# Pairing the value products of two branches, and laying the compression inputs out by a token's place in its stretch of 16

## The chip, the cores and the metric

The kernel runs on one core of a Trainium2 chip. The metric is the device time of one execution in microseconds (us). Three runs of the kernel before gave 1453.22, 1454.13 and 1451.1 us, a median of 1453.22.

## The reference, cut to what matters

The program is a decoder trunk of two layers over 512 tokens of width 1024, in float32. Layer 0 mixes tokens with sparse attention in three branches, layer 1 with a recurrence (RWKV-7). Each layer also attends to 256 memory tokens and ends with a SwiGLU feed-forward block. The change touches three places of it:

```python
def _compress(kv, pos, w1, w2):            # keys (kvi 0) and values (kvi 1)
    S = kv.shape[1]
    n_cmp = (S - CMP_BLOCK) // CMP_STRIDE + 1          # 31 blocks of 32 tokens, a step of 16
    idx = jnp.arange(n_cmp)[:, None] * CMP_STRIDE + jnp.arange(CMP_BLOCK)[None, :]
    blocks = kv[:, idx] + pos[None, None, :, None, :]
    hid = jax.nn.gelu(jnp.einsum('bnlgd,lde->bnge', blocks, w1))
    return jnp.einsum('bnge,ed->bngd', hid, w2)
...
        o_s = jnp.einsum('bgrqk,bgqkd->bqgrd', p_s.astype(vg.dtype), vg)   # selected branch
...
        o_w = jnp.einsum('bgrqk,bkgd->bqgrd', p_w.astype(vwc.dtype), vwc)  # window branch
...
    return jnp.einsum('bhsm,bmhd->bshd', p, v).reshape(B, S, MEM_WIDTH)    # memory attention
```

## The kernel before, in words

All large matrix products have a weight tile of 128x128 on the array and 512 token columns streaming through; each is done three times with operands split into a high and a low part (`pm` tiles; `nxh`, `wsp` and the like are those parts). Products that are not split are plain float32 and appear in the trace as two rows per product.

The program is first recorded as a list of operations with their dependences; `schedule` then simulates the engines with fixed costs (the function `cost`) and picks, engine by engine, the ready operation with the lowest number that fits in the buffers. What comes out is a fixed order for each engine: on the chip an engine executes its list strictly in that order. All operations carry line 517, where the list is emitted, so rows are told apart by tile names. `flex` operations may go to ScalarE (ACT) or VectorE (DVE), whichever the scheduler finds free first. The field `after` of an operation adds dependences that the data doesn't ask for. For TensorE (PE) the scheduler also knows how much of the array an operation uses (`colmode`: 128 or 64 columns) and prefers to stay in a mode within the bounds of `TILED`.

Layer 0 (`nsa`) works in four groups of three heads. For each group and each query tile `qt` of 128 tokens, the two branches `br` (selected, window) get their scores (`pa<-kh,qs` and `pa<-kl,qs`), bias and minimum on DVE, the exponential on ACT, the normalization on GpSimd (POOL, tile `p`); then PE transposes `p` (`ptr<-cf,p`), an eviction copies the transposes from PSUM to `ap` in SBUF (`copied`), and the value products follow (`po<-ap,vst`): 64 output rows, 384 columns, with `tile_position=(0, 64*br)`, so branch 0 uses columns 0 to 63 of the array and branch 1 columns 64 to 127. There are qt+1 key tiles, so 2, 4, 6 or 8 value products, 80 in all four groups (160 rows). In the recorded program the two branches of a key tile stand beside each other, but each of them waits only for its own eviction. `mem_attn` has the same shape with 512 columns: per head pair m, two key tiles with two heads each, products `pa<-mpt,mvs` (64 output rows, heads on the two halves of the array); it runs four times, twice in each layer, 16 products.

The compression (`compress`) runs twice, for keys (kvi 0) and values (kvi 1). For each of two weight tiles m, a large product `pm` is evicted to `kcf` on DVE (two head groups of 64 rows, 512 tokens), and DMAs issued by SyncE's queue (SP) copy it into `kc2`: rows 0 to 63 hold a group's tokens, rows 64 to 127 the same shifted by one token, 8 DMAs per compression. Sixteen products `pa<-kc,wraw` (128x128 weights from `cw1`) read every 16th column: 128 columns for the 4 groups of 32 stretches and one column of positions, 129 in all, written by POOL from `cpos`. The `cost` function doubles the price of float32 products with 129 columns. Then follow the GELU (`cgt`), the second product (`cw`), and the block-diagonal copies (`cdi`).

Of the kernel before, what the change touches and what calls it, by code (L numbers as in the profile page):

```python
# [11 lines left out]
F32 = mybir.dt.float32  # L12
# [3 lines left out]
ALU = mybir.AluOpType  # L16
# [545 lines left out]
def cost(eng, meth, args, kw, outs, ins):  # L562
# [8 lines left out]
    if eng == "tensor":  # L571
# [5 lines left out]
        if x.dt == F32:  # L577
            t = n * 4 / 2.4 + 5
            if n == 129:
                t *= 2  # L580
            if m <= 64 and w.shape[0] <= 64:
                t = 58.0 if n <= 64 else 55.0
            elif n <= 64 and m <= 64:
                t = 54.0 if m > 32 else 27.0
            elif n >= 256 and m == 64:
                t = n * 2 / 2.4 + 5
            elif n < 128:
                t = max(t, 215.0 if m > 64 else 112.0 if m > 32 else 60.0)
        elif x.dt == F32R:
            t = n / 2.4 + 13  # L590
        else:
            t = n / 2.4 + 2 if m > 64 else 16
# [27 lines left out]
class B:  # L620
# [205 lines left out]
    def copied(self, out, ps):  # L826
        self.nc.flex(("scalar", "copy", (out, ps), {}), ("vector", "tensor_copy", (out, ps), {}))
# [21 lines left out]
    def mem_attn(self, m, qm, kv, ot):  # L849
# [31 lines left out]
        for mt in range(2):  # L881
            pts = []
            for i in range(2):
# [6 lines left out]
                self.copied(pts[i], pt)  # L890

            for i in range(2):
                nc.tensor.matmul(po[64 * i:64 * i + 64], vs[mt][:, 2 * m + i], pts[i],
                                 start=mt == 0, stop=mt == 1, tile_position=(0, 64 * i))
# [67 lines left out]
    def nsa(self, xt):  # L962
# [37 lines left out]
        def compress(kvis):  # L1000

            for kvi in kvis:


                flat = nc.tile([128, 2080], F32, "kc2", "kc2", 1)
                kc2 = flat[:, 0:2048].rearrange("p (g n) -> p g n", g=4)
                cpos = self.sm("cpos", [128, 16])
                nc.sync.dma_start(cpos, self.a["cpos"][kvi])
                nc.gpsimd.tensor_scalar(out=flat[:, 2048:2080:2], in0=cpos, scalar1=1.0,
                                        scalar2=1.0, op0=ALU.mult, op1=ALU.mult)  # L1010
                for m in range(2):
# [3 lines left out]
                    nc.vector.tensor_tensor(out=kcf, in0=ps, in1=R, op=ALU.mult)  # L1015
                    for half in range(2):
                        hs = slice(64 * half, 64 * half + 64)
                        g = 2 * m + half
                        nc.sync.dma_start(kc2[0:64, g, :], kcf[hs])
                        nc.sync.dma_start(kc2[64:128, g, 0:511], kcf[hs, 1:512])  # L1020
                ps = self.ax_ps()
                for c in range(2):
                    cw = self.wraw(self.a["cw1"][kvi][:, c * 1024:c * 1024 + 1024])
                    for l in range(8):
                        ll = 8 * c + l
                        w = cw[:, l * 128:l * 128 + 128]
                        nc.tensor.matmul(ps[:, :129], w, flat[:, 2 * ll:2 * ll + 2049:16],
# [151 lines left out]
        for g in range(G):  # L1179
# [15 lines left out]
            for qt in range(4):  # L1195
# [35 lines left out]
                aps = []  # L1231
                for kt in range(qt + 1):
                    for br in range(2):
# [5 lines left out]
                        self.copied(aps[-1], pt)  # L1239

                for kt in range(qt + 1):
                    for br in range(2):
                        nc.tensor.matmul(po[64 * br:64 * br + 64], vst[kt][:, br, g],
                                         aps[2 * kt + br], start=kt == 0, stop=kt == qt,
                                         tile_position=(0, 64 * br))
# [586 lines left out]
```

## Time and profile before

| | us |
|---|---|
| profiled execution, time | 1453.28 |
| its span | 1451.5 |
| PE busy | 1418.1 (98%) |
| DVE busy | 834.2 (57%) |
| ACT busy | 656.4 (45%) |
| POOL busy | 125.8 (9%) |
| mean granted TensorE clock | 0.993 |

The span is what the profile covers; the execution's own time is 1.8 us longer. Busy shares are shares of the span. The mean duration of a PE row holds some 0.16 us of pipeline latency that overlaps the next row, so what a row costs the engine is the distance from its start to the start of the next. Times in rows are microseconds from the start of the span.

### The profile page before, as it was taken

The numbers are of one execution on the slowest core, as the hardware profiler recorded it, in microseconds if no ns is written. First come the engines' busy times: TensorE is split into PE (matmuls) and PEld (weight loads), VectorE is DVE, ScalarE is ACT, GpSimd is POOL, SyncE is SP. The second block draws the span as 40 slices with busy tenths as digits, with TensorE's granted clock in tenths as the row PEclk, the third lists the DMA queues.
The fourth block names the chain that finished last, engine by engine and source line by source line (L and its number), as shares of the span: only waits on it lengthen the run. The fifth ranks groups of instructions, "written<-read, shape, count | busy, mean of one in ns | idle before, by whom it ended". The sixth has DMA issues, their size and how long they took to land.

```text
span 1451.5 us, 24917 instructions
## 1 busy us (share of the span) xinstructions
PE 1418.1 (98%) x9914; PEld 1131.7 (78%) x9914; DVE 834.2 (57%) x1735; ACT 656.4 (45%) x1443; POOL 125.8 (9%) x214
## 2 busy tenths in 40 slices
PE   9999999999999999999999999999899999999997
PEld 7867776778888888888777777866688888888886
DVE  7754478756444544544559968786474444434435
ACT  7654477644223432333546565684452323312314
POOL 0232125310000000000000010210000000000003
PEclk9999999999999999999999999999999999999998
DMA  7333522232233323223213011012232333322212
GB/s 251 109 83 102 154 65 80 96 109 91 80 120 102 122 96 102 93 97 115 97 62 103 24 54 53 12 50 89 75 102 80 109 102 101 101 89 86 88 58 74
DMA packets 50228, 133.39 MB, mean 92 GB/s; under 512 B 6208, under 2 KB 14784, under 8 KB 50112
## 3 DMA queue, kind: packets, MB, share of 16 engines
q1 hardware_dynamic: 50112, 131.80, 28.5%
q8 instruction: 78, 1.28, 0.4%
q14 instruction: 38, 0.31, 0.1%
HBM read 122.34 MB, written 4.19 MB: 87 GB/s over the span
## 4 chain that ended last, share of the span: by engine, by line
PE 87%; DVE 4%; ACT 3%; DMA 2%; issue 1%; POOL 1%; SPq 0%; ACTq 0%; POOLq 0%; DVEq 0%
PE pm L517 68%; PE pa L517 13%; PE po L517 2%; PE pv L517 2%; PE ptr L517 2%; PE py L517 1%; DVE gram L517 1%; POOL p L517 1%; ACT tm L517 1%; DMA bias<-bias 0%; PE pg L517 0%; ACT gyo L517 0%; SPq L517 0%; POOL mp L517 0%; ACT p L517 0%
## 5 line engine op out<-in xcount | busy, mean ns | idle before, releaser
L517 PE MATMUL pm<-fxh,wsp 128*128 128x512 f32 x1408 | 435.1, 389 | 0.0
L517 DVE TENSOR_TENSOR wsp<-wraw,wsp 128x512 fp32r<-128x512 f32 (+2 forms) x432 | 280.8, 663 | 63.7 <-ACT wsp L517 61.7
L517 PEld LDWEIGHTS pm<-fxh,wsp 128*128 128x128 f32 x1408 | 264.1, 188 | 54.7
L517 ACT CAST wsp<-wraw 128x512 fp32r<-128x512 f32 (+2 forms) x432 | 238.6, 592 | 96.7 <-DMA wraw<-w_fi 66.2
L517 PE MATMUL pm<-fxl,wsp 128*128 128x512 f32 x704 | 274.0, 389 | 0.0
L517 PE MATMUL pm<-hxh,wsp 128*128 128x512 f32 (+1 forms) x736 | 220.4, 380 | 0.0
L517 PEld LDWEIGHTS pm<-hxh,wsp 128*128 128x128 f32 x736 | 136.3, 188 | 26.2
L517 PEld LDWEIGHTS pm<-fxl,wsp 128*128 128x128 f32 x704 | 132.1, 188 | 27.4
L517 PE MATMUL pm<-hxl,wsp 128*128 128x512 f32 (+1 forms) x368 | 139.4, 380 | 0.0
L517 DVE TENSOR_TENSOR xt<-pm,xt 128x512 f32<-128x512 f32 (+1 forms) x80 | 50.4, 637 | 133.5 <-PE pm L517 133.3
L517 PE MATMUL pm<-wxh,wsp 128*128 128x512 f32 x368 | 126.1, 408 | 0.0
L517 ACT CAST hxh<-hu 128x512 fp32r<-128x512 f32 x44 | 27.3, 621 | 207.6 <-DVE hu L517 207.6
L517 DVE TENSOR_TENSOR hu<-pm,R 128x512 f32<-128x512 f32 x44 | 30.4, 692 | 121.6 <-PE pm L517 121.6
L517 ACT ACTIVATE hg<-hg 128x512 f32<-128x512 f32 x44 | 27.8, 632 | 153.4 <-DVE hg L517 153.4
L517 PE MATMUL pm<-oxh,wsp 128*128 128x512 f32 x256 | 86.8, 411 | 1.2 <-ACT mp L517 0.7
L517 PE MATMUL pm<-nxh,wsp 128*128 128x512 f32 x256 | 86.4, 405 | 1.6 <-ACT nxh L517 1.1
L517 POOL TENSOR_SCALAR p<-p,ars,gate 128x128 f32<-128x128 f32 (+3 forms) x96 | 72.0, 765 | 173.8 <-DVE ars L517 107.3
L517 PEld LDWEIGHTS pm<-wxh,wsp 128*128 128x128 f32 x368 | 67.4, 188 | 18.5 <-issue 5.8
L517 PEld LDWEIGHTS pm<-hxl,wsp 128*128 128x128 f32 x368 | 69.2, 188 | 13.1
L517 DVE TENSOR_TENSOR hg<-pm,R 128x512 f32<-128x512 f32 x44 | 30.4, 692 | 80.4 <-PE pm L517 75.5
L517 PE MATMUL pm<-wxl,wsp 128*128 128x512 f32 x184 | 74.6, 405 | 0.0
L517 ACT ACTIVATE p<-p,amn 128x128 f32<-128x128 f32 (+3 forms) x96 | 53.4, 559 | 19.4 <-DVE amn L517 18.9
(313 smaller groups left out, 2104.8 us busy)
## 6 DMA issues: line engine op xcount, KB each, us to landing
wraw<-w_fi SPq DMA_DIRECT2D x88, 512.0 KB, 3.3
wraw<-w_fo SPq DMA_DIRECT2D x24, 512.0 KB, 3.3
wraw<-w_rw SPq DMA_DIRECT2D x23, 512.0 KB, 3.4
wraw<-w_fo SPq DMA_DIRECT2D x24, 384.0 KB, 3.0
wraw<-w_o SPq DMA_DIRECT2D x16, 512.0 KB, 3.3
wraw<-w_nsa SPq DMA_DIRECT2D x12, 512.0 KB, 3.7
xt<-xT SPq DMA_DIRECT2D x16, 256.0 KB, 5.1
bias<-bias SPq DMA_DIRECT2D x12, 256.0 KB, 4.6
```

The costliest lines, as they stand in the source:

```text
L517: o.ret = getattr(getattr(nc, o.eng), o.meth)(*[res(x) for x in o.args], **{k: res(v) for k, v in o.kw.items()})
```

## The change

Three edits. The value products of both attention kinds get `after=`: every product of a pair waits for the evictions of both partners, so the scheduler sees the two become ready together. The evictions (`copied`) return their operation for that. The compression input `kc2` becomes [128, 8, 132]: for each of 8 places l it holds 128 columns (4 groups of 32 stretches), where rows 0 to 63 hold the even token 2l of a stretch and rows 64 to 127 the odd token 2l+1; then two position columns and two zero columns. A stretch's second half of a block is the same tile read one column further on (`c:c + 130`). DVE writes `kcf` in that order (by place), reading PSUM and the row of scales `R` at a step of 16 tokens; the DMAs now move runs of 32 floats, half the bytes, in as many DMAs as before. The products have 130 columns, adjacent ones. The doubling in `cost` is gone.

```diff
@@ cost
         if x.dt == F32:
             t = n * 4 / 2.4 + 5
-            if n == 129:
-                t *= 2
@@ copied
-        self.nc.flex(("scalar", "copy", (out, ps), {}), ("vector", "tensor_copy", (out, ps), {}))
+        return self.nc.flex(("scalar", "copy", (out, ps), {}), ("vector", "tensor_copy", (out, ps), {}))
@@ mem_attn
-            pts = []
+            pts, done = [], []
...
-                self.copied(pts[i], pt)
+                done.append(self.copied(pts[i], pt))
...
                 nc.tensor.matmul(po[64 * i:64 * i + 64], vs[mt][:, 2 * m + i], pts[i],
-                                 start=mt == 0, stop=mt == 1, tile_position=(0, 64 * i))
+                                 start=mt == 0, stop=mt == 1, tile_position=(0, 64 * i),
+                                 after=done)
@@ compress
-                flat = nc.tile([128, 2080], F32, "kc2", "kc2", 1)
-                kc2 = flat[:, 0:2048].rearrange("p (g n) -> p g n", g=4)
+                kc2 = nc.tile([128, 8, 132], F32, "kc2", "kc2", 1)
                 cpos = self.sm("cpos", [128, 16])
                 nc.sync.dma_start(cpos, self.a["cpos"][kvi])
-                nc.gpsimd.tensor_scalar(out=flat[:, 2048:2080:2], in0=cpos, scalar1=1.0,
-                                        scalar2=1.0, op0=ALU.mult, op1=ALU.mult)
+                nc.gpsimd.memset(kc2[:, :, 130:132], 0.0)
+                for j in range(2):
+                    nc.gpsimd.tensor_scalar(out=kc2[:, :, 128 + j], in0=cpos[:, 8 * j:8 * j + 8],
+                                            scalar1=1.0, scalar2=1.0, op0=ALU.mult, op1=ALU.mult)
...
-                    nc.vector.tensor_tensor(out=kcf, in0=ps, in1=R, op=ALU.mult)
+                    k4 = kcf.rearrange("p (j e n) -> p j e n", j=8, e=2)
+
+                    def by_place(t):
+                        return t.rearrange("p (n j e) -> p j e n", j=8, e=2)
+                    nc.vector.tensor_tensor(out=k4, in0=by_place(ps), in1=by_place(R), op=ALU.mult)
...
-                        nc.sync.dma_start(kc2[0:64, g, :], kcf[hs])
-                        nc.sync.dma_start(kc2[64:128, g, 0:511], kcf[hs, 1:512])
+                        for e in range(2):
+                            nc.sync.dma_start(kc2[64 * e:64 * e + 64, :, 32 * g:32 * g + 32],
+                                              k4[hs, :, e, :])
...
-                        nc.tensor.matmul(ps[:, :129], w, flat[:, 2 * ll:2 * ll + 2049:16],
+                        nc.tensor.matmul(ps[:, :130], w, kc2[:, l, c:c + 130],
                                          start=ll == 0, stop=ll == 15)
@@ nsa, value products of both branches
-                        self.copied(aps[-1], pt)
+                        done.append(self.copied(aps[-1], pt))
...
                                          aps[2 * kt + br], start=kt == 0, stop=kt == qt,
-                                         tile_position=(0, 64 * br))
+                                         tile_position=(0, 64 * br),
+                                         after=done[2 * kt:2 * kt + 2])
```

What this does to the order, at the three places that matter. First, PE in front of the first compression (`kc_...` is the compression's input): before, from the value products in front of it:

```order
L517 MATMUL po<-ap,vst 64x384 x3
L517 MATMUL pm<-nxh,wsp 128x512
L517 MATMUL pm<-nxl,wsp 128x512
L517 MATMUL pm<-nxh,wsp 128x512 x2
L517 MATMUL pm<-nxl,wsp 128x512
L517 MATMUL pm<-nxh,wsp 128x512 x2
L517 MATMUL ptr<-cf,p 128x128 x3
L517 MATMUL pm<-nxl,wsp 128x512
L517 MATMUL ptr<-cf,p 128x128 x3
L517 MATMUL pm<-nxh,wsp 128x512
L517 MATMUL ptr<-cf,p 128x128
L517 MATMUL pa<-kc_1118,wraw 128x129 x16
```

and PE at the same place now:

```order
L517 MATMUL po<-ap,vst 64x384 x4
L517 MATMUL pm<-nxh,wsp 128x512
L517 MATMUL pa<-kc_67,wraw 128x130 x16
L517 MATMUL ptr<-cf,p 128x128 x18
```

In both versions twelve score products (`pa<-kh,qs` and `pa<-kl,qs`, 128x384) stand directly ahead of the value products, and ahead of those the last product of the `pm` that `kcf` is evicted from. Between that `pm` and the compression stood 12 score products, 3 value products, 9 `pm` products and 7 transposes; now 12, 4, 1 and none. In front of the second compression it was 21 `pm` products and 13 transposes, and is 11 and 12.

Second, PE at the first query tile of the third group (`po_2164` and `po_2220` are that tile's value output). Before, its two products stand ten rows apart:

```order
L517 MATMUL po_2164<-ap_2130,vst_798 64x384
L517 MATMUL ptr_2157<-cf_101,p_2127 128x128
L517 MATMUL pa_2135<-cf_101,scT_2153 128x128
...
L517 MATMUL pm_2177<-mxh_293,wsp_1815 128x256
L517 MATMUL po_2164<-ap_2173,vst_798 64x384
L517 MATMUL pm_2177<-mxl_313,wsp_1815 128x256
```

and now:

```order
L517 MATMUL pm_2094<-mxh_337,wsp_1856 128x256
L517 MATMUL po_2220<-ap_2176,vst_800 64x384
L517 MATMUL po_2220<-ap_2208,vst_800 64x384
L517 MATMUL pm_2094<-mxh_347,wsp_1842 128x256
```

Runs of adjacent value products had the lengths 1, 2, 9, 8 in the first group, 3, 3, 6, 8 in the second, 1, 1, 4, 1, 5, 8 in the third and 1, 1, 10, 8 in the fourth; they are now 1, 2, 8, 9 and then three times 2, 4, 6, 8. In the first group branch 1's values come later than branch 0's, and its first products stay apart. The products of `mem_attn` stood as 1 and 3 in three of four calls and as 4 in one; they now stand as 4 in all.

Third, SP's queue, with the first compression's DMAs. Before:

```order
L517 DMA wraw<-cw 128x1024
L517 DMA kc_1118<-kcf 64x512
L517 DMA kc_1118<-kcf 64x511
L517 DMA kc_1118<-kcf 64x512
...
L517 DMA wraw<-w_nsa 128x1024 x3
L517 DMA wraw<-w_mk 128x1024
```

and now:

```order
L517 DMA wraw<-cw 128x1024
L517 DMA kc_67<-kcf 64x8x32 x8
L517 DMA wraw<-w_nsa 128x1024 x3
L517 DMA wraw<-w_mk 128x1024
L517 DMA kc_1584<-kcf 64x8x32 x4
```

The count of DMAs and their place are the same; each now moves 64 x 8 runs of 128 bytes in place of 64 runs of 2 KB. In the second compression a weight load (`w_mv`) stood between the last DMAs and now stands behind them.

## Rows read from the trace of the kernel before

**Rows 1.** The page's busy times (part 1) and slices (part 2).

```profile
PE 1418.1 (98%) x9914; PEld 1131.7 (78%) x9914; DVE 834.2 (57%) x1735; ACT 656.4 (45%) x1443; POOL 125.8 (9%) x214
PE   9999999999999999999999999999899999999997
PEclk9999999999999999999999999999999999999998
```

**Rows 2.** The chain that ended last (part 4), by engine, and who PE waited for in the whole span: total us, times, longest.

```profile
PE 87%; DVE 4%; ACT 3%; DMA 2%; issue 1%; POOL 1%; SPq 0%; ACTq 0%; POOLq 0%; DVEq 0%
...
PE ptr L517 <- POOL p L517: 4.6, 5, 1.6
PE pa L517 <- DVE lth L517: 2.8, 4, 1.5
PE pg L517 <- ACT gyo L517: 2.4, 1, 2.4
PE pa L517 <- DMA kl<-kl: 2.4, 2, 2.1
...
PE pa L517 <- DMA kc<-kcf: 0.8, 1, 0.8
```

**Rows 3.** The timeline of PE at both compressions: start, us, instruction; in brackets the idle time before it and what ended it.

```profile
125.67 7.20 PE L517 MATMUL pa<-kc,wraw 128*128 128x129 f32 x32
132.70 1.38 PE L517 MATMUL ptr<-cf,p 128*128 128x128 f32 x11
...
161.97 7.26 PE L517 MATMUL pa<-kc,wraw 128*128 128x129 f32 x32 [0.84 <-DMA kc<-kcf]
168.88 0.58 PE L517 MATMUL pm<-nxh,wsp 128*128 128x512 f32 x1
```

**Rows 4.** The timeline of PE at a float32 product with adjacent columns (the sums of squares), and all rows of that tile: duration ns min/median/max.

```profile
28.21 1.05 PE L517 MATMUL pa<-cf,sq 128*128 128x128 f32 x8
...
L517 PE MATMUL pa<-cf,sq x56: 270/275/554, 28.2 to 1443.7; 128*128 128x128 f32 x56
```

**Rows 5.** The timeline of PE at runs of 8, 4, 3 and 1 value products, each with the row behind it.

```profile
97.03 2.80 PE L517 MATMUL po<-ap,vst 128*64 128x384 f32 x16
99.77 0.50 PE L517 MATMUL pm<-nxh,wsp 128*128 128x512 f32 x1
...
219.19 1.51 PE L517 MATMUL po<-ap,vst 128*64 128x384 f32 x8
220.64 0.33 PE L517 MATMUL ptr<-cf,p 128*128 128x128 f32 x1
...
112.34 1.50 PE L517 MATMUL po<-ap,vst 128*64 128x384 f32 x6
113.78 0.44 PE L517 MATMUL ptr<-cf,p 128*128 128x128 f32 x2
...
189.11 0.86 PE L517 MATMUL po<-ap,vst 128*64 128x384 f32 x2
189.90 0.33 PE L517 MATMUL ptr<-cf,p 128*128 128x128 f32 x1
```

**Rows 6.** The timeline of PE at the products of memory attention: a call with runs of 1 and 3, and the call with a run of 4.

```profile
252.90 1.07 PE L517 MATMUL pa<-mpt,mvs 128*64 128x512 f32 x2
253.90 0.38 PE L517 MATMUL pa<-kl,qs 128*128 128x256 f32 x1
...
254.39 1.93 PE L517 MATMUL pa<-mpt,mvs 128*64 128x512 f32 x6
256.25 0.33 PE L517 MATMUL ptr<-cf,p 128*128 128x128 f32 x1
...
946.54 2.07 PE L517 MATMUL pa<-mpt,mvs 128*64 128x512 f32 x8
948.55 0.44 PE L517 MATMUL pa<-tQ,tT 64*64 64x64 f16 x16
```

**Rows 7.** The timeline of PE, DVE and SP at the first compression's last eviction: the last `pm` product, the first score product behind it and the first value products; `kcf`; the four DMAs. Below, the landing of all 16 DMAs after their issue, us min/median/max.

```profile
118.85 0.39 PE L517 MATMUL pm<-nxh,wsp 128*128 128x512 f32 x1
119.08 0.33 PE L517 MATMUL pa<-kh,qs 128*128 128x384 f32 x1
121.28 0.54 PE L517 MATMUL po<-ap,vst 128*64 128x384 f32 x2
...
119.35 0.69 DVE L517 TENSOR_TENSOR kcf<-pm,R 128x512 f32<-128x512 f32 x1 [4.62 <-PE pm L517]
...
120.07 2.39 SPq L517 DMA_DIRECT2D kc<-kcf  x4
...
DMA to landing us min/median/max: 2.2/2.3/4.1
```

**Rows 8.** DMA issues with many pieces (count, KB each, median us from issue to landing), and the queue's line: packets, MB, share of 16 engines over the span. `out` has 256 runs of 1 KB, `kc` 64 of 2 KB.

```profile
out<-xout SPq DMA_DIRECT2D x8, 256.0 KB, 2.4
kc<-kcf SPq DMA_DIRECT2D x8, 128.0 KB, 2.3
...
q1 hardware_dynamic: 50112, 131.80, 28.5%
```

**Rows 9.** Busy times in two stretches of layer 0: PE, PEld, DVE, ACT, POOL, then PEclk, DMA share, GB/s.

```profile
180.00:240.00 60.00, 56.70 (x335) 41.75 (x335) 46.30 (x150) 44.56 (x125) 20.62 (x25) 1.00 0.25 73
240.00:300.00 60.00, 58.30 (x315) 39.89 (x311) 43.58 (x110) 40.87 (x114) 27.59 (x40) 1.00 0.32 105
```

More of the change, by code (lines that the diff above doesn't have):

```diff
@@ L1230, in nsa @@
                                                 op0=ALU.mult, op1=ALU.mult)
-                aps = []
+                aps, done = [], []
                 for kt in range(qt + 1):
```

## The prediction, made before the changed kernel ran

> **What bounds the kernel now.** I read the page's busy times first, then the chain that ended last and PE's waits, then PE's timeline at the places that the change touches. PE is busy 98% of the span at a granted clock of nine tenths or more in every slice, and no other engine passes 57% [rows 1]. The chain that ended last lies on PE for 87% [rows 2]. PE's longest waits in total are 4.6 us (for POOL's normalization), and each other line is under 3 us; the wait for the compression's input is 0.8 us, once [rows 2]. So a microsecond less of PE work should be worth close to a microsecond, unless the shortened list of PE runs into an operand that isn't there yet. That second half is what the sum below is really about.
>
> The reader should see in the timelines that what counts on PE is the distance between starts. The compression's 32 rows take 132.70 - 125.67 = 7.03 us the first time and 168.88 - 161.97 = 6.91 us the second [rows 3], 0.22 us per row. Eight rows of a float32 product with 128 adjacent columns take 1.05 us from the first start to the last end, 0.275 us of it the last row: (1.05 - 0.275) / 7 = 0.111 us per row [rows 4]. Nearly the same count of columns at a step of 16 costs twice as much.
>
> **Compression products.** 32 products of two rows are replaced by 32 of the same kind with 130 columns, adjacent ones. By the adjacent row, 64 x 0.111 x 130/128 = 7.2 us in place of 13.94: 6.7 us less. The bounds: 6.9 us less if the two columns more are free, and nothing, if the doubling hangs on a count above 128 and not on the step. I take 6.7, since the value products, with 384 columns, show no doubling (next part).
>
> **Value products.** A run of 8 takes 99.77 - 97.03 = 2.74 us, a run of 4 220.64 - 219.19 = 1.45, so each product more costs 0.323 us, and 0.15 us go for entering and leaving the run; that is 384 columns at 0.84 ns for one row, though each product has two. So two neighbours on the two halves of the array run at the same time. A single one takes 189.90 - 189.11 = 0.79 us and a run of 3 takes 1.44, as long as 4 [rows 5]. A product without a partner costs two slots of 0.323 us where a paired one costs one. By the run lengths in the order (front section), the second to fourth group had 22, 24 and 22 slots (3, 3, 6, 8 are 4 + 4 + 6 + 8, and so on) and now have 20 each: 8 slots less, 2.6 us; and 12 runs for 14, 0.3 us. The first group keeps its unpaired ones, since branch 1's values come late; I count nothing there (bounds: 0.6 us either way, two slots). Together 2.9 us less.
>
> In memory attention, runs of 1 and 3 take 253.90 - 252.90 = 1.00 and 256.25 - 254.39 = 1.86 us; the call that already had a run of 4 takes 948.55 - 946.54 = 2.01 [rows 6]. That is 0.85 us less in each of three calls, 2.5 us.
>
> The waits that this edit adds cost PE nothing where other work stands ahead of the later eviction, and the order has moved such work ahead (score products, transposes, `pm`). Queued behind a waiting product is everything of PE, as on any wait. If that cover is gone, each of the 40 + 8 pairs can wait for one eviction; the trace shows PE losing 4.6 us on POOL in the whole span and less on any other line [rows 2], so I bound this by -1 to +5.5 us (lines of that size doubled, or a little of them relieved) and take 0, as the evicting engines are at 57% and 45% [rows 1].
>
> The sum so far: 6.7 + 2.9 + 2.5 = 12.1 us less.
>
> **The compression's input, now late.** This is the term on the other side. In the first compression, the last `pm` product is followed on PE from 119.08 us; `kcf` is evicted from 119.35 for 0.69 us; SP issues four DMAs from 120.07 for 2.39 us, so the last at about 121.86, and it lands 2.3 us later: 124.2 us [rows 7]. PE used to arrive at 125.67 [rows 3] and found the data there. Now only 12 score products (121.28 - 119.08 = 2.20 us, [rows 7]), a run of 4 (1.45, [rows 5]) and one `pm` product (119.08 - 118.85 = 0.23, [rows 7]) stand between: PE arrives at 119.08 + 3.88 = 122.96, and waits 1.2 us. For the second, 11 `pm` products and 12 transposes are 11 x 0.23 + 12 x 0.11 = 3.85 us against the same chain of 5.1: 1.25 us. The wait of 0.84 us that was there [rows 3] is contained in that. Net, 1.2 + 1.25 - 0.84 = 1.6 us more, with every link as before.
>
> Two links are not as before. The DVE eviction reads PSUM and SBUF at a step of 16 floats. No DVE row of before does that: between 0 and one more 0.69 us [rows 7], as PE's read at that step doubled [rows 3, 4]. I take half, 0.35 us twice: 0.7 us. [...] No row here shows DVE at such a step.
>
> The DMAs move half the bytes in 512 runs of 128 bytes each where there were 64 of 2 KB. Below: half the bytes may take half the issue's 2.39 us off, 1.2 us per compression. Above: the queue's 50112 packets took 28.5% of 16 engines' span, 132 ns each at 2.6 KB on average [rows 8]; if a short run cost as much, 4 x 32 runs on each engine are 16.9 us in place of 16 x 0.132 = 2.1, so 14.8 us more per compression. The nearest row is `out`, whose 256 runs (16 per engine) land in 2.4 us where 64 runs land in 2.3 [rows 8]: 0.1 us for 12 runs more, so 0.25 us for 28 more, and up to 1.0 when four DMAs queue behind each other. I take 0.6 us twice: 1.2 us.
>
> [...]
>
> GpSimd writes the position and zero columns with three instructions for one. It is 9% busy [rows 1], and they wait for nothing new: nothing.
>
> **The sum.** 12.1 - 1.6 - 0.7 - 1.2 = 8.6 us less. The profiled execution took 1453.28 us, its span of 1451.5 and 1.8 around it, and lies at the median of the runs, 1453.22. So 1444.7 us.
>
> **Rivals.**
>
> Late input for good (slower). If short runs cost what a mean packet costs, the two compressions wait 2 x 14.8 us longer: 12.1 - 1.6 - 0.7 - 29.6 is a loss of 19.8 us, 1473 us. It decides from the point where the extra wait of a compression exceeds (12.1 - 2.3) / 2 = 4.9 us, so 2.1 + 4.9 = 7.0 us for 128 runs, 55 ns per run. For it: SP's order puts all four DMAs of an eviction directly in front of the products that need them, and PE has nothing left in between. Against it: `out` with four times the runs lands only 0.1 us later [rows 8].
>
> The gain comes back as waits (smaller gain). Softmax in layer 0 runs through DVE, ACT and POOL, and in the stretch from 180 to 240 us PE has 3.3 us of 60 idle already, while DVE and ACT are at 46 and 45 us of 60 [rows 9]. If PE is ahead by several us there and meets the same `p` from POOL, the upper bound of 5.5 us is lost: 1444.7 + 5.5 = 1450.2 us. Against it: these engines have room, and nothing of their work grew.
>
> The step is not the cause. If products with more than 128 columns are slow whatever their step, the 6.7 us stay: 1444.7 + 6.7 = 1451.4 us, no change within what can be told. Against it: rows 5, where 384 columns cost 0.84 ns each.
>
> The pairs are made in the order and don't run together. A product's weights must be loaded when its partner streams; if half of the new pairs ran singly, 2.7 us are lost: 1447.4 us. Against it: every adjacent pair that I could read in the second to fourth group did run together, as the run of 8 shows [rows 5].
>
> **How the numbers follow.** What a measurement of this kernel can tell from no change is about 0.2%, 2.9 us; so faster means under 1450.3. The forecast gets 0.68, with a range of its own from 1441 to 1448 (the DMA term from -1.2 to +1.0 per compression, the eviction from 0 to 0.69). The pairs that don't run together get 0.06, the gain that comes back 0.13, the step 0.05, late input for good 0.08, of which a part, with a run at 30 to 55 ns, still ends below or near the time of before. Faster: 0.68 + 0.06 + half of 0.13 + a little of the others = 0.82; same 0.12; slower 0.06. The range for 8 in 10 leaves out the largest delays: 1440.5 to 1451.
>
> **What would show it.** Right: 32 rows of `kc` in about 3.6 us, run lengths of value products 2, 4, 6, 8 at 0.323 us each, memory attention at 2.0 us in all four calls, and a wait of PE for `kc` of some 2 us in front of each compression. Wrong: `kc` rows at 0.22 us; a DMA of `kc` that lands 5 us after its issue or more; a `kcf` row far above 1.4 us; or PE's waits for POOL's `p` above some 10 us in total.

## The result, and the profile after

The changed kernel took 1438.85 us (median of 4 executions, 1436.98 to 1441.52) against 1452.99 us for the kernel before (median of 4, 1451.1 to 1454.13): a ratio of 0.9911, with a 95% interval of 0.9895 to 0.9926. It is faster, as forecast, but by 14.1 us where 8.6 were forecast, and its time lies below the range of 1440.5 to 1451. The profiled execution took 1437.71 us with a span of 1435.9.

The page's busy times and the granted clock by slices after the change:

```profile
PE 1401.5 (98%) x9914; PEld 1122.1 (78%) x9914; DVE 834.7 (58%) x1733; ACT 658.0 (46%) x1445; POOL 124.6 (9%) x218
...
PEclk9999999999999999999999999999999999999999
```

PE has 16.6 us less of busy time than in [rows 1] (1418.1 - 1401.5), the same count of instructions, and is still busy for 98%. The other engines stand where they stood. So nearly all of the gain is PE work that runs in less time, and hardly any is a wait that went.

Who PE waited for in the whole span (total us, times, longest):

```profile
PE pa L517 <- DMA kc<-kcf: 3.1, 2, 1.6
PE pg L517 <- ACT gyo L517: 2.4, 1, 2.4
PE ptr L517 <- POOL p L517: 2.1, 5, 1.2
...
PE pa L517 <- DVE lth L517: 1.5, 4, 0.8
```

Against [rows 2], the wait for the compression's input grew from 0.8 to 3.1 us and is now the longest in total. The one for POOL's `p` fell from 4.6 to 2.1, and the one for `lth` from 2.8 to 1.5, its longest from 1.5 to 0.8.

PE's timeline at both compressions, as in [rows 3]:

```profile
120.98 0.49 PE L517 MATMUL pm<-nxh,wsp 128*128 128x512 f32 x1
122.95 3.81 PE L517 MATMUL pa<-kc,wraw 128*128 128x130 f32 x32 [1.47 <-DMA kc<-kcf]
126.60 0.60 PE L517 MATMUL ptr<-cf,p 128*128 128x128 f32 x4
...
155.60 3.81 PE L517 MATMUL pa<-kc,wraw 128*128 128x130 f32 x32 [1.61 <-DMA kc<-kcf]
159.24 0.27 PE L517 MATMUL ptr<-cf,p 128*128 128x128 f32 x1
```

32 rows now take 126.60 - 122.95 = 3.65 and 159.24 - 155.60 = 3.64 us, where they took 7.03 and 6.91. In front of each stands the new idle time in brackets.

The links of the chain ahead of them, as in [rows 7]: all rows of the eviction and of the transfers by tile (duration ns min/median/max, first and last start), and the landing of the transfers.

```profile
L517 DVE TENSOR_TENSOR kcf<-pm,R x4: 1042/1047/1056, 108.6 to 150.2; 128x512 f32<-128x512 f32 x4
...
L517 SPq DMA_DIRECT2D kc<-kcf x16: 590/634/1288, 109.7 to 153.2; - x16
...
DMA to landing us min/median/max: 2.1/2.3/3.5
```

And SP's timeline, the four issues of the first compression's last eviction:

```profile
118.61 2.62 SPq L517 DMA_DIRECT2D kc<-kcf  x4
```

The eviction takes 1.047 us instead of 0.69, the four issues 2.62 instead of 2.39, and the landing is as before: 2.3 us.

Memory attention, as in [rows 6], the first call of each layer:

```profile
242.68 1.94 PE L517 MATMUL pa<-mpt,mvs 128*64 128x512 f32 x8
244.54 0.88 PE L517 MATMUL ptr<-cf,p 128*128 128x128 f32 x6
...
936.07 1.94 PE L517 MATMUL pa<-mpt,mvs 128*64 128x512 f32 x8
937.93 0.44 PE L517 MATMUL pa<-tQ,tT 64*64 64x64 f16 x16
```

Each call is one run of four pairs and takes 1.86 us from its first start to the next row's (244.54 - 242.68); so do the other two, at 287.00 and 962.20.

**Where the time went, by stages.** Three starts in PE's timeline mark the same work in every kernel: the first `pa<-kl,qs`, the first `pm<-fxh` of layer 0 (its feed-forward part begins) and the first `pm<-fxh` of layer 1. The distances between them, in us, in the profiles of both kernels and of the experiments told below:

| kernel | start to `kl` | `kl` to layer 0's `fx` | `fx` to layer 1's `fx` | to PE's last start |
|---|---|---|---|---|
| before | 43.26 | 285.30 | 744.84 | 370.26 |
| before, again | 45.35 | 285.27 | 745.78 | 369.46 |
| after | 42.63 | 275.15 | 740.57 | 369.45 |
| after, again | 42.46 | 275.37 | 740.64 | 369.48 |
| layout alone | 44.42 | 277.50 | 743.23 | 369.48 |
| value products alone | 43.84 | 282.65 | 742.23 | 369.49 |
| memory attention alone | 45.36 | 283.90 | 740.59 | 369.47 |
| after, layer 1 as before | 45.12 | 275.19 | 744.65 | 370.23 |
| after, input planned late | 43.54 | 275.79 | 740.71 | 370.24 |
| after, idle time filled | 43.44 | 275.41 | 739.62 | 369.49 |
| after, both of these | 45.07 | 274.67 | 739.46 | 369.47 |
| before, idle time filled | 42.21 | 285.37 | 743.14 | 369.43 |
| before, steps 16 and 2 | 45.58 | 281.51 | 743.48 | 369.42 |
| after, steps 1 and 4 | 45.08 | 278.98 | 740.58 | 370.23 |

The second column repeats within 0.3 us for the same order of work; the first varies from one execution to the next by some 3 us whatever the kernel. The change is worth 285.30 - 275.15 = 10.15 us in layer 0, and 744.84 - 740.57 = 4.27 us in layer 1, where the forecast had only one call of memory attention, 0.85 us. Layer 1 is where most of the missing gain lies.

There the granted clock differs. Two stretches of layer 1 before the change (busy us of PE, PEld, DVE, ACT, POOL; granted clock; DMA share; GB/s):

```profile
985.00:1000.00 15.00, 13.50 (x213) 9.12 (x213) 12.42 (x22) 8.14 (x17) 0.00 (x0) 0.89 0.21 70
...
1045.00:1060.00 15.00, 10.90 (x37) 8.41 (x36) 8.45 (x18) 6.36 (x12) 0.00 (x0) 0.77 0.11 36
```

And the stretches with about the same work after it:

```profile
970.00:985.00 15.00, 14.18 (x229) 10.34 (x231) 13.75 (x24) 8.16 (x18) 0.00 (x0) 1.00 0.16 49
...
1030.00:1045.00 15.00, 10.90 (x43) 8.50 (x42) 9.50 (x19) 7.01 (x13) 0.00 (x0) 0.89 0.10 37
```

If PE's work there goes by the clock, 15 us at a mean granted clock of 0.89 are 1.65 us lost, at 0.77 3.45 us. Before, the two stretches lose 1.65 + 3.45 = 5.1 us, after 0 + 1.65: an estimated difference of 3.45 us that is no work at all. PE's timeline before, at the idle time ahead of each stretch and at the second stretch and its end:

```profile
986.92 0.31 PE L517 MATMUL pa<-chh,lth 64*64 64x64 f16 x8 [1.50 <-DVE lth L517]
...
1047.30 0.63 PE L517 MATMUL pa<-cf,ry 128*128 128x128 f32 x4 [1.72 <-DVE ry L517]
1050.31 0.80 PE L517 MATMUL pg<-zgxh,wsp 128*128 128x512 f32 x1 [2.38 <-ACT gyo L517]
1050.90 0.63 PE L517 MATMUL pg<-zgxl,wsp 128*128 128x512 f32 x1
1051.33 0.63 PE L517 MATMUL pg<-zgxh,wsp 128*128 128x512 f32 x1
...
1057.07 0.40 PE L517 MATMUL pm<-oxl,wsp 128*128 128x512 f32 x1
1057.30 0.39 PE L517 MATMUL pm<-oxh,wsp 128*128 128x512 f32 x1
```

In such a stretch the products of 512 columns start 0.43 us apart (1051.33 - 1050.90) in place of 0.23 (1057.30 - 1057.07): the clock's lower level, granted at 0.50 in place of 1.00. By the trace it held from 988.01 to 991.42 us and from 1049.45 to 1056.28, so the second stretch began 0.86 us before the idle time ahead of `pg` ended. The page's row PEclk, of 36 us per digit, showed a 9 for all of this in [rows 1].

### The profile page after: what moved, and what is told of

The parts are those of the page before. It is cut to its first block, busy times and chain, and to the rows that moved or that the text cites. A ratio compares the mean times of both kernels' runs of the same rounds, so it can differ in the third digit from the quotient of the medians.

```text
span 1435.9 us, 24914 instructions
## 1 busy us (share of the span) xinstructions
PE 1401.5 (98%) x9914; PEld 1122.1 (78%) x9914; DVE 834.7 (58%) x1733; ACT 658.0 (46%) x1445; POOL 124.6 (9%) x218
## 3 DMA queue, kind: packets, MB, share of 16 engines
q8 instruction: 78, 1.28, 0.4%
## 4 chain that ended last, share of the span: by engine, by line
PE 88%; DVE 4%; ACT 3%; DMA 1%; issue 1%; POOL 1%; SPq 0%; ACTq 0%; POOLq 0%; DVEq 0%
PE pm L517 69%; PE pa L517 12%; PE po L517 2%; PE pv L517 2%; PE ptr L517 2%; PE py L517 1%; POOL p L517 1%; DVE gram L517 1%; DMA kl<-kl 1%; ACT gyo L517 1%; ACT tm L517 0%; PE pg L517 0%; POOL mp L517 0%; SPq L517 0%; DMA kc<-kcf 0%
## 5 line engine op out<-in xcount | busy, mean ns | idle before, releaser
L517 POOL TENSOR_SCALAR p<-p,ars,gate 128x128 f32<-128x128 f32 (+3 forms) x96 | 68.8, 732 | 170.0 <-DVE ars L517 105.4
```

Of the source, the lines that this page charges most:

```text
L517: o.ret = getattr(getattr(nc, o.eng), o.meth)(*[res(x) for x in o.args], **{k: res(v) for k, v in o.kw.items()})
```

## Experiments

The diffs are cut to what matters, with constants written in.

**The parts alone.** Three kernels each make one part of the change to the kernel before.

Layout alone: the tile `kc2`, its eviction and transfers as changed, without the waits for both evictions.

```diff
-flat[:, 2 * ll:2 * ll + 2049:16]
+kc2[:, l, c:c + 130]
```

> Only the compression's new layout; no value product waits for its partner's eviction. Theory 'sum of parts' (the layout is worth its 6.7 us of product time less the wait for late input): kc rows at 0.111 us, two waits for kc of 1.2 to 1.7 us each, layer 1 in the order of before, so 4 to 5 us less than before: ratio 0.9965 to 0.9975. Rival 'the layout alone brings more' (its shorter DMAs and products relieve other waits of layer 0): 7 us less or more, ratio 0.995 or lower. Rival 'late input eats it': ratio above 0.998.

Measured: 1443.73 us, ratio 0.994 (0.9927 to 0.9954), so some 8.7 us less by the ratio. The second expectation holds, not the first: this is above the sum of the forecast's terms for this part (6.7 - 3.5 = 3.2). The stages say why: 7.80 us in layer 0. The planner's new order put some products side by side without being told to: value products take 32.49 us from start to start in place of 33.05, memory attention 9.60 in place of 10.59, 1.55 us together that belong to the other parts. And in layer 1, whose order is that of before, one of the two stretches at the low clock did not come: from 975 to 990 us, behind a wait of 1.50 us for `lth`, the granted clock was 1.00.

Value products alone:

```diff
 nc.tensor.matmul(po[64 * br:64 * br + 64], vst[kt][:, br, g],
                  aps[2 * kt + br], start=kt == 0, stop=kt == qt,
-                 tile_position=(0, 64 * br))
+                 tile_position=(0, 64 * br),
+                 after=done[2 * kt:2 * kt + 2])
```

> Only the value products of the two branches wait for both evictions; compression and memory attention as before. Theory 'sum of parts': 8 slots of 0.323 us less and fewer runs, 2.9 us, ratio 0.998. Rival 'the reordering itself relieves waits for POOL's p in layer 0': 5 us less or more, ratio 0.9965 or lower. Rival 'the new waits cost what the pairs save': ratio 0.9995 to 1.001.

Measured: 1448.65 us, ratio 0.9981 (0.9969 to 0.9994), and 2.65 us in layer 0, against 2.9 forecast.

Memory attention alone:

```diff
 nc.tensor.matmul(po[64 * i:64 * i + 64], vs[mt][:, 2 * m + i], pts[i],
-                 start=mt == 0, stop=mt == 1, tile_position=(0, 64 * i))
+                 start=mt == 0, stop=mt == 1, tile_position=(0, 64 * i),
+                 after=done)
```

> Only memory attention's products wait for both evictions. Theory 'layer 1 order' (what the prediction missed is in layer 1, whose order only this edit changes: less idle in front of the third group and shorter stretches at half clock behind it): 2.5 us of products plus 3 to 4 us in layer 1, ratio 0.9955 to 0.9965, and in the trace at most one stretch of 3.4 us at half clock in layer 1. Rival 'chance windows' (the half-clock stretches of layer 1 come and go from execution to execution whatever the order): 2.5 us, ratio 0.998, half-clock stretches as likely as before.

Measured: 1448.23 us, ratio 0.9973 (0.9964 to 0.9982): 3.9 us by the ratio, between the two expectations. In layer 0 it gives 1.40 us. In layer 1, 744.84 - 740.59 = 4.25 us, all that the whole change gives there. So layer 1's gain comes through this edit alone, and it is more than a call of memory attention can hold (1.1 us).

**Layer 1 as before.** The changed kernel, with memory attention in layer 1 left unpaired.

```diff
-                        self.mem_attn(j, qm[j], kv, ot)
+                        self.mem_attn(j, qm[j], kv, ot, False)
```

> The changed kernel, but in layer 1 memory attention's products wait each for its own eviction, so from the start of the first feed-forward block PE's order is that of before. Theory 'layer 1 order': it is 4 to 5 us slower than the changed kernel (0.85 us of products, the rest idle time and half clock), ratio to before 0.9935 to 0.9945, and its trace shows two stretches at half clock as before's. Rival 'chance windows': within 1.5 us of the changed kernel, ratio 0.991 to 0.992.

Measured: 1445.09 us, ratio 0.9946 (0.9932 to 0.996), so some 5 us slower than the changed kernel by the ratios to the kernel before (0.9946 against 0.9911). Layer 0 keeps its whole gain (275.19), layer 1 loses all of it (744.65). The wait for `lth` is back, and behind it the low clock. PE's timeline, and then the windows as above:

```profile
978.52 0.31 PE L517 MATMUL pa<-chh,lth 64*64 64x64 f16 x8 [1.50 <-DVE lth L517]
```

```profile
970.00:985.00 15.00, 13.50 (x170) 9.41 (x169) 13.32 (x23) 4.54 (x12) 0.00 (x0) 0.89 0.00 1
...
1030.00:1045.00 15.00, 10.94 (x68) 8.03 (x67) 7.63 (x16) 5.98 (x12) 0.00 (x0) 0.87 0.12 37
1045.00:1060.00 15.00, 15.00 (x62) 12.23 (x61) 12.49 (x21) 8.91 (x16) 0.00 (x0) 0.91 0.28 86
```

Lost to the clock: 15 x (0.11 + 0.13 + 0.09) = 4.95 us, as before the change. In the changed kernel PE stands idle for 0.15 us in front of the same `lth` products:

```profile
973.91 0.65 PE L517 MATMUL pa<-chh,lth 64*64 64x64 f16 x16 [0.15 <-DVE lth L517]
```

This left two theories of the low clock: that TensorE's idle time brings it, or that it comes at moments of its own and the changed kernel's executions had fewer of them.

**Both kernels again.** A second profile of each.

> The changed kernel once more, on the chip of the three runs behind it, as their base. Expected: 1437 to 1441 us, ratio 0.991, 3.1 us of waits for the compression's input, and one stretch at half clock of 3.4 us near 1036 us besides the one at the very end. If those stretches come by chance of the moment, this profile has them at other places than the first one.

> The kernel before once more, for a second profile. If idle stretches bring the half clock, it stands at the same two places again (behind 987 and behind 1047 us, within a few us for the start), 3.4 or 6.8 us long; if it comes by chance of the moment, at others.

Measured: the changed kernel 1438.9 us, ratio 0.9907 (0.9891 to 0.9924), with one stretch at the low clock in the same place (0.89 from 1030 to 1045 us). The kernel before 1455.33 us, with stretches in the same two places, the first now twice as long:

```profile
985.00:1000.00 15.00, 13.28 (x151) 9.32 (x151) 11.85 (x21) 5.50 (x12) 0.00 (x0) 0.77 0.08 27
...
1045.00:1060.00 15.00, 10.91 (x45) 8.36 (x42) 8.87 (x18) 6.24 (x12) 0.00 (x0) 0.77 0.21 64
```

In these two pairs of profiles the places belong to the kernel, and the lengths vary.

**Idle time filled, after.** The changed kernel with products that nobody reads in the two idle stretches at the end of layer 1's attention (1.72 us for `ry`, 2.38 us for `gyo`), behind which its one stretch at the low clock came.

```diff
+            if m0 == 4 and q == 1:
+                self.idle(zgh, 6, vr)
             for c in range(4):
-                nc.tensor.transpose(pt[:, c * 128:c * 128 + 128],
+                tr = nc.tensor.transpose(pt[:, c * 128:c * 128 + 128],
...
+            if m0 == 4 and q == 1:
+                self.idle(zgh, 9, tr)
```

> The changed kernel, with 6 products more ahead of the last transposes of the attention's output in layer 1 and 9 more behind them, whose results nobody reads: 15 x 0.227 = 3.4 us of work for TensorE in the 1.72 and 2.38 us in which it stands idle at 1031.8 and 1034.1 us. Theory (the half clock follows from TensorE standing idle): no stretch at half clock near 1036 to 1042 us, mean granted clock 0.002 higher, and 1.7 us faster than the changed kernel (3.4 us at half the rate), ratio 0.990. Rival (the half clock comes at its own times, whatever TensorE does): a stretch of 3.4 us stays, and the time is that of the changed kernel or up to 1 us longer, ratio 0.991 to 0.992.

PE's timeline at the place, and then the window:

```profile
1031.56 1.52 PE L517 MATMUL fill<-zgxh 128*128 128x512 f32 x6
1033.89 0.63 PE L517 MATMUL pa<-cf,ry 128*128 128x128 f32 x4 [0.82 <-DVE ry L517]
1034.28 2.33 PE L517 MATMUL fill<-zgxh 128*128 128x512 f32 x9
1036.91 0.50 PE L517 MATMUL pg<-zgxh,wsp 128*128 128x512 f32 x1 [0.30 <-ACT gyo L517]
```

```profile
1030.00:1045.00 15.00, 13.88 (x62) 10.84 (x61) 9.85 (x20) 8.22 (x16) 0.00 (x0) 1.00 0.22 70
```

With idle times of 0.82 and 0.30 us left, the clock stays at its full level (1.00 in the window), and layer 1 takes 1.0 us less than in the changed kernel (739.62 against 740.64). 15 idle products more make a stage shorter. The whole time does not show it: 1438.78 us, ratio 0.9905 (0.989 to 0.992), because 1 us is less than the start varies by.

**Idle time filled, before.** The same on the kernel before, in front of the `lth` products, its order otherwise unchanged.

```diff
+        if self.units == 6:
+            ps = self.ax_ps("fill")
+            for _ in range(12):
+                nc.tensor.matmul(ps[:, 0:128], self.ident, self.ident, start=True, stop=True, after=lev)
```

> The kernel before in its own order, with 12 transposes of a constant more on TensorE (12 x 0.107 = 1.28 us, results unused) a few products ahead of the lth products of the third group in layer 1, before which it stands idle for 1.50 us at 985.4 us. Theory (the half clock follows from TensorE standing idle): that idle stretch falls to some 0.2 to 0.6 us and no stretch at half clock follows near 988; the one behind 1047 us stays, since its two idle stretches are left as they are. Mean granted clock 0.001 to 0.002 above the kernel before; time 1 to 2 us less, ratio 0.999. Rival (the order in which kinds of products alternate there, or the moment, brings it): a stretch at half clock stays near 988 with the idle time gone, ratio 1.000 to 1.001.

PE's timeline at the place, and then the windows:

```profile
982.62 2.84 PE L517 MATMUL fill<-cf 128*128 128x128 f32 x24
...
986.99 0.31 PE L517 MATMUL pa<-chh,lth 64*64 64x64 f16 x8
```

```profile
985.00:1000.00 15.00, 15.00 (x244) 10.83 (x242) 12.67 (x22) 9.43 (x20) 0.00 (x0) 1.00 0.26 78
...
1045.00:1060.00 15.00, 11.81 (x46) 9.51 (x47) 10.08 (x17) 8.83 (x16) 0.00 (x0) 0.89 0.13 39
```

Each filling product made two rows (24 in 2.84 us, the last row's end included), so they took 2.6 us and not 1.28, and the idle time in front of `lth` is gone. So is the stretch at the low clock behind it, while the other one, whose idle time was left alone, stays. Layer 1 takes 743.14 us, 1.7 less than in the first profile of the kernel before and 2.6 less than in the second. The time, 1451.85 us at a ratio of 0.9994 (0.9982 to 1.0005), is 1.2 us lower but not to be told from no change. One profile could be chance, as the tally below shows. The granted clock of all executions says more: it was 0.9955 on the mean of 11, against 0.9940 for 15 of the kernel before measured beside them, as expected. As the order was that of before, this speaks against the rival (the order of the products brings the low clock).

Over all profiles, the tally is: the 1.50 us in front of `lth` were followed by a stretch at the low clock in 4 of 6 profiles (not in those of the layout alone and of the value products alone), and no profile without that idle time had one there (8 of 8). The pair of 1.72 and 2.38 us was followed by one in all 12 profiles that had it, and in neither of the 2 in which it was filled. So at these two places the idle time goes together with the low clock, and filling it keeps the clock up.

But idle time of this length is not enough. In layer 0, waits of 1.64 to 1.66 us for `p` (five profiles) and of 2.06 to 2.40 us ahead of the first `kl` (nine profiles) were followed by no such stretch, and twelve waits of 1.46 to 1.63 us for `kc` by one. A wait of 2.16 us for `p`, in the two kernels with the late input below, was followed by one both times. What tells these places apart is not shown.

**The late input.** The changed kernel, with the planner told a later landing for `kc2`, so that it puts more products ahead of the compression; and this together with the filled idle time.

```diff
-                    fin = dma_free + 1900
+                    fin = dma_free + (LATE if isinstance(o.args[0], AV) and o.args[0].t.name == "kc2"
+                                     else 1900)
+LATE = 4000
```

> The changed kernel, with the planner told that the transfers into kc2 land 4.0 us after their queue is free instead of 1.9, so that it puts more products of other work ahead of the compression. Theory (the late input is a matter of the order alone, the 3.1 us of waits are a loss that is left in the changed kernel): the wait for kc falls from 3.1 to under 0.5 us and the time by about 3 us, ratio 0.989. Rival (the products that are moved ahead are missing later, so that the wait goes elsewhere): the wait for kc falls too, but the time stays within 1 us of the changed kernel, ratio 0.991.

> Both edits of the two runs before at once. If both theories hold, 3 + 1.7 us below the changed kernel, ratio 0.988; if one holds, its part alone; if neither, 0.991.

Of the first of the two, PE's timeline at the first compression and at the longest idle time behind it in layer 0, and then its waits:

```profile
125.05 3.73 PE L518 MATMUL pa<-kc,wraw 128*128 128x130 f32 x32
...
223.48 0.90 PE L518 MATMUL ptr<-cf,p 128*128 128x128 f32 x3 [2.16 <-POOL p L518]
```

```profile
PE ptr L518 <- POOL p L518: 5.6, 9, 2.2
PE pa L518 <- DMA kl<-kl: 2.5, 2, 2.1
```

The wait for `kc` is gone, and layer 0 takes 275.79 us instead of 275.37: the wait for `p` has grown from 2.2 us in the second profile of the changed kernel to 5.6. The rival holds: the 3.1 us are not for the taking by order alone. Not all of it is waits, though. The idle time of layer 0 in all fell from 9.91 to 8.85 us, but behind the new idle time of 2.16 us for `p` a stretch at the low clock came (products of 512 columns start 0.43 us apart at 224.60 and 225.03 us), which takes up to 1.7 us by the reckoning above. The time was 1440.43 us, ratio 0.9916 (0.9901 to 0.9931).

Both edits together gave 1438.8 us, ratio 0.9907 (0.9892 to 0.9922), the time of the changed kernel. In the profiles the two middle stages took 274.67 + 739.46 us, 1.9 less than in the second profile of the changed kernel, but the start took 2.6 more. No version here is faster than the changed kernel by more than can be measured.

**The step or the odd count.** The change replaces 129 columns at a step of 16 by 130 adjacent ones, two things at once. Two kernels part them (each reads other columns in its second compression).

```diff
-flat[:, 2 * ll:2 * ll + 2049:16]
+(flat[:, 2 * ll:2 * ll + 2065:16], flat[:, 2 * ll:2 * ll + 257:2])[kvi]
...
-kc2[:, l, c:c + 130]
+(kc2[:, l, c:c + 129], kc2.rearrange("p j n -> p (j n)")[:, ll:ll + 517:4])[kvi]
```

> The kernel before, where the first compression reads 130 columns at a step of 16 elements instead of 129, and the second one 129 columns at a step of 2 (other columns than the reference asks for: the value compression is wrong). Theory (the step makes the row of the float32 product take twice as long): 130 columns at step 16 take 0.22 us a row, as 129 did; the rows at step 2 say whether a small step costs too, 0.111 if only far columns cost, 0.22 if every step does. Rival (the odd number of columns makes it, since the change went from 129 to 130 at the same time): 130 columns at step 16 take 0.112 us, 129 at step 2 take 0.22.

> The changed kernel, where the first compression reads 129 adjacent columns instead of 130, and the second one 130 columns at a step of 4 elements (other columns than the reference asks for: the value compression is wrong). Theory (the step): 129 adjacent columns take 0.111 us a row; step 4 lies between 0.111 and 0.22 and says where the cost begins. Rival (the odd number): 129 adjacent columns take 0.22 us, 130 at step 4 take 0.112.

The timeline of PE at both compressions, first of the kernel with steps 16 and 2, then of the one with steps 1 and 4:

```profile
129.04 7.30 PE L517 MATMUL pa<-kc,wraw 128*128 128x130 f32 x32
136.17 1.27 PE L517 MATMUL ptr<-cf,p 128*128 128x128 f32 x10
...
163.68 3.85 PE L517 MATMUL pa<-kc,wraw 128*128 128x129 f32 x32
167.28 0.71 PE L517 MATMUL pm<-nxh,wsp 128*128 128x512 f32 x2
```

```profile
125.31 3.81 PE L517 MATMUL pa<-kc,wraw 128*128 128x129 f32 x32 [1.48 <-DMA kc<-kcf]
128.95 2.13 PE L517 MATMUL ptr<-cf,p 128*128 128x128 f32 x18
...
157.96 7.66 PE L517 MATMUL pa<-kc,wraw 128*128 128x130 f32 x32 [1.63 <-DMA kc<-kcf]
165.44 0.29 PE L517 MATMUL ptr<-cf,p 128*128 128x128 f32 x1
```

Per row: step 16 with 130 columns (136.17 - 129.04) / 32 = 0.223 us, step 2 with 129 columns 0.113, step 1 with 129 columns 0.114, step 4 with 130 columns 0.234. The count plays no part and the step is the cause: 2 costs next to nothing, 4 as much as 16. (Steps between were not run.) What lies behind this is not shown.

The rows at step 4 hold a second finding. From 159.67 to 163.08 us, in their midst, the granted clock was 0.5; here is a window inside that stretch:

```profile
160.00:163.00 3.00, 3.00 (x15) 3.00 (x14) 0.00 (x0) 0.00 (x0) 0.00 (x0) 0.50 0.06 12
```

In the trace these rows start 0.23 us apart there as they do ahead of it and behind it, while products of 512 columns slowed from 0.23 to 0.43 us in such stretches. Layer 0 bears it out: it is 3.8 us longer than in the changed kernel (278.98 - 275.15), which is what the step adds to the 32 rows (7.48 - 3.64). So this one stretch at the low clock cost nothing, and the time of a row at step 4 did not go by TensorE's clock.

## Why the prediction was right and wrong

By the two profiled executions, 1453.28 and 1437.71 us, the change is worth 15.6 us. The terms, in us (work from start to start of the rows on PE, so with the time that a product takes from the next one):

| term | forecast | measured | from |
|---|---|---|---|
| compression products | -6.7 | -6.6 | 64 rows, 13.94 to 7.30 |
| value products | -2.9 | -2.8 | 160 rows, 33.05 to 30.22 |
| memory attention | -2.5 | -3.1 | 32 rows, 10.59 to 7.47 |
| wait for the compression's input | +3.5 | +2.2 | 0.84 to 3.08 |
| other idle time in layer 0 | 0 | -0.7 | 8.22 to 9.74 in all, less the line above |
| low clock in layer 1 | no term | -3.4 | windows, 5.1 to 1.65 lost |
| start, up to the first `kl` | no term | -0.6 | 43.26 to 42.63, varies |
| rest | | -0.5 | last stage -0.8, layer 1 the other way |
| sum | -8.6 | -15.6 | |

**The step that failed** is the one in the first part: PE's granted clock was taken as nine tenths or more in every slice [rows 1] (the last one shows an 8), and from that a microsecond of PE work as a microsecond of time. The sum had no term for the clock. Slices of 36 us hide that the kernel before lost, by the reckoning above, 5.1 us in two windows of layer 1, both at idle times of PE that stand in the waits: 1.5 us for `lth` and 2.4 for `gyo` [rows 2]. The waits were read as prices of their own size; the low clock behind them cost about as much again in that profile. The prediction did say that memory attention in layer 1 becomes shorter by one call, and did not follow what the moved order does there: the `lth` products no longer wait, so the stretch behind them goes. Three runs bear this out: memory attention alone moves layer 1 by 4.25 us; undoing it in layer 1 alone gives the 4.1 us back; and with that idle time filled in the kernel before, its order kept, the stretch did not come and the mean granted clock of the executions rose.

It is a chance more than a fixed sum, and the profile of before had more of it than most. Over the six profiles whose layer 1 has the order of before with nothing filled, that stage took 742.23 to 745.78 us, 744.0 on the average; over the five with the order of after, 740.57 to 740.71. Of the 3.4 us between, 1.1 are memory attention and 0.4 shorter idle time, so the clock is worth some 2 us on the average. All executions together agree: the mean granted clock was 0.9942 over 22 of the kernel before, 0.9948, 0.9942 and 0.9938 in the three kernels beside it that keep its layer 1, and 0.9961, 0.9962 and 0.9955 with the layer 1 of after (memory attention alone, and the changed kernel twice). Such a mean takes in the end of the span, where the clock is low (0.50 from 1441.99 us in the profile of before, from 1429.03 in that of after), so it is not turned into microseconds here.

By the medians 5.5 us were missing in the forecast (14.1 less 8.6). Some 2 us of them are the clock in layer 1, 1.3 the late input, 0.7 other idle time, 0.6 memory attention. The last stage adds up to 0.8: it took 370.2 us in the profile of before and in three others, and 369.4 to 369.5 in the other ten. In the profile of before the clock falls to 0.50 ahead of the last products (by the trace, at 1441.99 us, where the last sums of squares start at 1442.03), in that of after behind them (at 1429.03, and 1426.94). That the fall came early in the other three as well is an estimate from the time of this stage. The profile of after lies 1.1 us below its median.

**Compression products**: right, to a tenth, and the rival that the step is not the cause is ruled out by its own test (129 columns at step 1, 130 at step 16).

**Value products**: right in sum and in mechanism. The pairs run together, and the loads of their weights, 0.14 us each, run beside the rows that stream (by the trace of after, from 119.92 us in a run that starts at 119.54); alone, the edit gave 2.65 us in layer 0.

**Memory attention**: the mechanism was right, the size short by 0.6. The call that had run as four pairs already was counted as unchanged at 2.01 us, but it takes 1.86 now, and so do the others.

**The late input**: the right sign and place, too large by 1.3. The waits of 1.47 and 1.61 us were forecast as 4.35 together. The eviction's 0.35 us is what came (1.047 - 0.692), but by luck: it was the middle of the bounds, and the upper end, 0.69 us more, did not come. The term for the DMAs' short runs was mis-sized: 0.6 each time, where the issue of four grew by 0.23 (2.62 - 2.39) and the median landing not at all (2.3 us both). That is some 0.7 of the 1.3. In the first compression PE also came 0.26 us later than reckoned, 4.14 us behind the start of the first score product in place of 3.88. The rival of an input that is late for good falls with the landing of 2.3 us at runs of 128 bytes. The experiment with the late input adds that this wait and the one for `p` share one slack: taken at one place (3.1 us for `kc`, to nothing), most of it comes back at the other (2.2 to 5.6 us for `p`), and the low clock behind it took the rest, by the estimate of up to 1.7 us.

**The waits for both evictions**: costed at nothing between bounds of -1 and +5.5; the idle time of layer 0 apart from `kc` fell by 0.7. The rival that the gain comes back as waits had 5.5 us of it; it did not happen, the wait for `p` even fell by 2.5 us.

## What to carry to other kernels

Look at the step of a product's moving operand: float32 columns at a step of 4 or 16 took two rows' time for one here (0.234 and 0.223 us), and at a step of 1 or 2 did not (0.114 and 0.113). Laying them out afresh cost half an eviction more (1.047 us for 0.692), 0.23 us of issue and nothing in landing (2.3 us both), and a wait for the input that other work no longer covered. A wait of TensorE of one or two microseconds can cost more than itself, by the clock behind it (the 1.50 us for `lth` in the profile of before stood ahead of 3.41 us at 0.50, an estimated 1.7 us lost): look in windows of 15 us, not in the page's slices, and expect the price to vary from one place and one execution to the next. A change of order moves such waits in stages that it doesn't touch in itself, so compare kernels stage by stage between marks of equal work.

## What the runs showed of the hardware that was not expected

A stretch of idle time of TensorE as short as 1.5 us was followed, in 4 of 6 profiles, by products at a granted clock of 0.50 in place of 1.00; two of 1.72 and 2.38 us within 5 us, with four transposes between, in 12 of 12. Waits of the same lengths in layer 0 were mostly not followed by any. Products whose results are thrown away, in their place, kept the clock at its full level (1.00 from 1030 to 1045 us) and made the stage shorter by 1.0 us although 15 of them were added. DVE, reading PSUM and SBUF at a step of 16 floats and writing adjacent ones, took 1.047 us where adjacent reads took 0.692: a factor of 1.5, where the same step cost TensorE a factor of 2 (0.223 us a row against 0.114). Float32 products that read their columns at a step of 4 took 0.23 us a row at either level of the clock, 0.50 and 1.00.
